# A hybrid convolution and state-space layer on one core: input sums and splits moved behind PSUM reads, and the last columns in two groups

## The chip, the cores and the metric

The kernel runs on one core of a Trainium2 chip. Time is device microseconds (us) of one execution; the median of three runs is quoted. Five engines work side by side, each through its own queue in order: TensorE (PE, with its weight loads as PEld), VectorE (DVE), ScalarE (ACT), GpSimd (POOL) and SyncE (SP), which here issues all DMAs.

## The reference, cut to what matters

One layer, for a prompt of 2048 tokens and a sample of 64, in fp32:

```python
h = rmsnorm(x, norm_in_w) * (1 + scale[:, None]) + shift[:, None]
proj = h @ w_in                       # 1024 -> 7184 columns
b_gate, c_gate, h_a, g_a, z, xbc_raw, dt_raw = jnp.split(proj, idx, axis=-1)
...                                   # short gated convolution -> y_a; chunked scan -> y_b
out = jnp.concatenate([y_a, y_b], axis=-1) @ w_out
x = x + gate[:, None] * out
y = rmsnorm(x, norm_f_w)
```

Outputs are y for both sequences and the final states of the convolutions and of the scan.

## The kernel before

**Two phases.** `phase_project` computes `h @ w_in` channel by token: 7 Strassen products in place of 8 block products, each operand split into a high and a low part (hi, lo in the one-pass fp32 format), so that a product is three matmuls. `phase_mix` then goes through 16 chunks of 128 prompt tokens (and the sample first): the scan, the output projection, the residual and the final norm.

**Items and slots.** `work` lists items, each 256 columns of w_in; items 0 to 27 are the first pass (tokens 0 to 1023, 512 columns to a matmul), items 28 to 55 the second (the other 1088 tokens, two units of 272 columns). An item has seven slots, one for each product; (24,2) is slot 2 of item 24. A slot's matmuls are 12 of 512 columns in the first pass, 24 of 272 in the second. The quarters and sums of the input that the products multiply (A11, S1, S2, S4, S3, A12, A22 for slots 0 to 6) stay in SBUF for a whole pass as tiles hi and lo, and are replaced for the second pass while item 27 and the first slots of item 28 run.

**What a slot issues,** in this order: its matmuls; activations that were due (`run_later`); the cast of the next item's weights (`w_hi`, ScalarE); the functions that `hooks` lists for the slot; some of the convolutions' work (`run_bg`); the low part of those weights and the next weight sums (`w_lo`, VectorE, one to three instructions, L233); then `evac`, the reads of PSUM: slots 0, 1, 2 into `keep` (ScalarE, L301), slots 3, 4, 5 added to `keep` (VectorE, L309), slot 6 (ScalarE, L307); then a function that `behind` lists. The order of a queue is the order of the code.

**Who waits for a PSUM read.** The matmuls of slot 2 add to the bank that slot 0 filled, so they wait for its `keep`; so slot 3 for slot 1 and slot 4 for slot 2. Slot 6 needs the bank read in slot 4. In the second pass slot 5 takes the banks read in slot 3, and slot 0 the banks read in slot 6 of the item before; unit 1 of (28,0) takes the bank that (27,6) leaves.

**Sums of the input.** `sums_in(i)` loads four blocks (tiles h_q) of one half of the channels from DRAM; `sums_step(i, n)` makes one sum on VectorE (L849, 128 x 1088) and stores it (hq_d). Both halves are done in items 23 to 25. `second_in(j, r)` loads what product j needs (tiles t_q, from hs_d or hq_d); `second(j)` casts it (two casts of 128 x 1088 on ScalarE, L171) and subtracts (two on VectorE, L172), then issues the load for product j+3.

**The last chunk.** Each chunk ends with `out_mm` for two halves of 512 columns; `take_b` scales, gates and adds each half (three VectorE instructions) and squares it with a sum (ScalarE); `end_rms` makes the root of the mean (VectorE, POOL), and `scale_out` multiplies all 1024 columns by it and by the final weight in one instruction (L1466), and stores them (L1467). For chunks but the last this runs beside the next chunk's work; after the last nothing is left to run beside it.

Of the kernel before, what the change touches and what calls it, by code (L numbers as in the profile page):

```python
# [8 lines left out]
F32 = mybir.dt.float32  # L9
F32R = mybir.dt.float32r  # L10
AF = mybir.ActivationFunctionType
ALU = mybir.AluOpType
# [15 lines left out]
def kernel(  # L28
# [8 lines left out]
    PE, ACT, DVE, POOL, SP = nc.tensor, nc.scalar, nc.vector, nc.gpsimd, nc.sync  # L37
# [3 lines left out]
    y_prompt, y_sample = y_prompt[0], y_sample[0]  # L41
# [35 lines left out]
    stats = pool(ctx, "stats", bufs=4)  # L77
# [16 lines left out]
    def rsqrt_mean(ss, n, out):  # L94
        ms = stats.tile([128, 1], F32, tag="ms", name="ms")
        DVE.tensor_scalar(out=ms[:n], in0=ss, scalar1=1.0 / D, scalar2=EPS, op0=ALU.mult, op1=ALU.add)
        POOL.tensor_tensor(out=out, in0=ms[:n], in1=mhalf[:n], op=ALU.pow)

    wo = {}

    def phase_project():
# [668 lines left out]
        def hook_at(t, fn):  # L770
            hook(t // 7, t % 7, fn)
# [55 lines left out]
        for gi in range(4):  # L827
            t0 = 19 * 7 + 1 + 8 * gi
# [8 lines left out]
        blocks = {}  # L837

        def sums_in(i):
            for n, (k0, o) in enumerate(((0, 0), (0, 544), (4, 0), (4, 544))):  # L840
                t = row(2 + n, [128, 2, 544], "h_q")
                SP.dma_start(out=t, in_=hs_d[:, k0 + 2 * i:k0 + 2 * i + 2, o:o + 544])
                blocks[n] = t

        def sums_step(i, n):
            a11, a21, a12, a22 = (blocks[x] for x in range(4))
            out, x, y, op = ((a22, a21, a22, ALU.add), (a21, a11, a21, ALU.subtract),
                             (a11, a22, a11, ALU.subtract), (a12, a12, a11, ALU.subtract))[n]
            DVE.tensor_tensor(out=out, in0=x, in1=y, op=op)  # L849
            SP.dma_start(out=hq_d[n, :, 2 * i:2 * i + 2, :], in_=out)  # L850

        for i, t0 in enumerate((23 * 7 + 6, 24 * 7 + 5)):
            hook_at(t0, lambda i=i: sums_in(i))
            for n in range(4):
                hook_at(t0 + 3 + n, lambda i=i, n=n: sums_step(i, n))

        tm = {}
        SOURCE = {"A11": (hs_d, 0, 0), "A12": (hs_d, 4, 0), "A22": (hs_d, 4, 544),
# [10 lines left out]
        def second(j):  # L869
            hi, lo = h_tile(PRODS[j], 544)  # L870
            for i, t in enumerate(tm.pop(j)):
                split(t, hi[:, 2 * i:2 * i + 2, :], lo[:, 2 * i:2 * i + 2, :])
            if j + 3 < 7:
                second_in(j + 3, (6, 2, 4)[j % 3])
# [1 line left out]
        hook(26, 0, lambda: second_in(0, 6))  # L876
        hook(26, 1, lambda: second_in(1, 2))
        hook(26, 2, lambda: second_in(2, 4))
        behind = {}
        for j, t, late in ((0, 1, 0), (1, 2, 0), (2, 4, 1), (3, 5, 1), (4, 6, 0), (5, 7, 0), (6, 9, 0)):  # L880
            if late:
                behind[27, t] = lambda j=j: second(j)
            else:
                hook_at(27 * 7 + t, lambda j=j: second(j))

        hook(30, 0, lambda: dt_project(1, 2))
        hook(30, 2, lambda: dt_gather(1))
# [49 lines left out]
        o = 0  # L937
        for ap in (conv_a_w[0], norm_a_w, conv_b_w[0], conv_b_b, norm_b_w, norm_in_w):
            n = ap.shape[0] * ap.shape[1] // 128
# [36 lines left out]
        for h, xs in enumerate(first):  # L976
            ss = x_ss()
            for i, (off, n, t) in enumerate(xs):
                ACT.activation(out=stage["A22"][:, 2 * (i % 2):2 * (i % 2) + 2, :].rearrange("p k t -> p (k t)"), in_=t,
                               func=AF.Square, accum_out=ss[:, i, 0:1])  # L980
# [150 lines left out]
        for n, (q, j) in enumerate((("A12", 3), ("A22", 3), ("A12", 2), ("A22", 2))):  # L1131
            plain_product(1, q, j)
            s4, t = (("S4", S), ("S3", S3))[n // 2]
# [92 lines left out]
        for g in range(2, last):  # L1226
            p = int(g >= NP0)
            slot_us = 2.75 if p == 0 else 3.05
            for s in range(7):
                now[0] = 7 * g + s  # L1230
                open_banks(p, g, s)
                product(p, g, s)
                run_later()
                if s == 1:
                    w_load(g + 2)
                if s == 2:
                    work[g][1]["begin"](p)
                tg, tj = (g, 6) if s == 0 else (g + 1, s - 1)
                if tg < last:
                    w_hi(tg, tj)  # L1240
                for fn in hooks.get((g, s), ()):
                    fn()
                cost = (W_COST[tj] if tg < last else 0.7) + (0.7 if 3 <= s <= 5 else 0.0) + (0.2 if p and s >= 3 else 0.0)
                credit = min(credit + slot_us - cost, slot_us)
                credit = run_bg(credit)
                if tg < last:
                    w_lo(tg, tj)
                elif s > 0:
                    last_w(s - 1)
                evac(p, g, s)  # L1250
                if (g, s) in behind:
                    behind[g, s]()
                if s == 4:
                    work[g][1]["done"](p, 1)
                if s == 6:
                    work[g][1]["done"](p, 0)
# [28 lines left out]
    def decay(c, hf):  # L1285
        h0, rb = hf * 8, loads[c, hf][1]
        lt = mix["sp1"].tile([128, 8, 128], F32, tag="lt", name="lt", bufs=2)
        for h in range(8):
            ACT.activation(out=lt[:, h, :], in_=rb[:, h, :], func=AF.Relu, scale=-1.0, bias=acum[:, c, h0 + h:h0 + h + 1])  # L1289
        ACT.activation(out=lt, in_=lt, func=AF.Exp, scale=-1.0)  # L1290
        held[c, hf] = lt

    def phase_mix():
        stack = ExitStack()
        psum = pool(stack, "ps2", bufs=5, space=bass.MemoryType.PSUM, reuse_waits="tile")
        sp = mix["sp"] = pool(stack, "sp", bufs=1, reuse_waits="tile")

        def bank(tag):
            return psum.tile([128, 512], F32, tag=tag, name=tag, bufs=5 if tag == "sd" else 3)
# [150 lines left out]
        def take_b(c, nn, t, ps, r, xr, ss):  # L1450
# [3 lines left out]
            DVE.tensor_tensor(out=xr[:n, s], in0=xr[:n, s], in1=t[:n], op=ALU.add)  # L1454
            ACT.activation(out=t[:n], in_=xr[:n, s], func=AF.Square, accum_out=ss[:n, nn:nn + 1])  # L1455

        def end_rms(c, ss):
            n = ntok(c)
            DVE.tensor_tensor(out=ss[:n, 0:1], in0=ss[:n, 0:1], in1=ss[:n, 1:2], op=ALU.add)
            rf = stats.tile([128, 1], F32, tag="rf", name="rf")  # L1460
            rsqrt_mean(ss[:n, 0:1], n, rf[:n])
            return rf
# [7 lines left out]
        n, va = NS_TOK, mix["va"]  # L1470
# [18 lines left out]
        vbh = split_act(vb, n, "vbh")  # L1489
# [4 lines left out]
        t0 = take_a(16, pa, ra)  # L1494
# [12 lines left out]
        t1 = take_a(16, pa, ra)  # L1507
# [8 lines left out]
        xr = prefetch_x(16)  # L1516
        gate = sp.tile([128, D], F32, tag="gate", name="gate")
        nf = sp.tile([128, D], F32, tag="nf", name="nf")
        SP.dma_start(out=gate, in_=g_d[1].partition_broadcast(128))
        SP.dma_start(out=nf, in_=norm_f_w.partition_broadcast(128))  # L1520
        ss = stats.tile([128, 2], F32, tag="fs", name="fs", bufs=2)
# [17 lines left out]
        pending = ends(16, t1, pb, rbs, xr, ss)  # L1539
        xr = prefetch_x(0)  # L1540
        for c in range(16):
            n, nxt, nx2 = 128, c + 1, c + 2
            more = nxt < 16
            vb = vb_of.pop(c)
            vbh = split_act(vb, n, "vbh")
            if more:
                prefetch(nxt, 1)
                prefetch_z(nxt, 1)
            if pending:
                pending[0]()  # L1550
            if more:
                va = prefetch_va(nxt)
                ssd1(nxt, 0)
            ra = inv_rms(sqa, n, "ra")
            if pending:
                pending[1]()
            split_dve(vb, n, vbh)
            square(vb, n)
            if pending:
                pending[2]()  # L1560
            sqb = sum_sq(vb, n, "vbh")
            if c == 0:
                SP.dma_start(out=gate, in_=g_d[0].partition_broadcast(128))
            if more:
                xr_next = prefetch_x(nxt)
            if not more:
                store_state()
            pa = out_mm(vah, 0, c, 0)
            if more:
                ssd2(nxt, 0)  # L1570
                decay(nxt, 1)
            t0 = take_a(c, pa, ra)
            if more:
                join1(nxt, 0)
                ssd1(nxt, 1)
                join2(nxt, 0)
                if nx2 < 16:
                    prefetch(nx2, 0)
                    prefetch_z(nx2, 0)
            pa = out_mm(vah, 0, c, 1)  # L1580
            rb_ = inv_rms(sqb, n, "rb")
            if more:
                ssd2(nxt, 1)
            t1 = take_a(c, pa, ra)
            if more:
                vah = split_act(va, n, "vah")
                split_dve(va, n, vah)
                square(va, n)
                join1(nxt, 1)
                sqa = sum_sq(va, n, "vah")  # L1590
                join2(nxt, 1)
                if nx2 < 16:
                    decay(nx2, 0)
            ss = stats.tile([128, 2], F32, tag="fs", name="fs", bufs=2)
            pb0 = out_mm(vbh, 8, c, 0)
            take_b(c, 0, t0, pb0, rb_, xr, ss)
            pb1 = out_mm(vbh, 8, c, 1)

            pending = ends(c, t1, pb1, rb_, xr, ss)
            if more:  # L1600
                xr = xr_next
        for f in pending:
            f()
        stack.close()

    with tc.manual_schedule():
# [30 lines left out]
```

## Time and profile before

| | |
|---|---|
| median of 3 runs | 1771.92 us (1771.9 to 1772.29) |
| the profiled execution, its own time | 1769.35 us |
| its span | 1767.5 us |
| busy share of the span | PE 97%, DVE 74%, ACT 47%, POOL 6% |
| chain of work that ended last | PE 86%, DVE 5%, DMA 4%, ACT 3% |
| lines of that chain | L276 (products) 54%, L1430 and L1437 (output projection) 21% |

The profile is of one execution. Busy time counts matmuls from start to end, and they overlap, so 97% does not mean that the engine runs at its peak; what matters is where it is not fed. The chain is followed back from the last instruction to what released each step.

### The profile page before, as it was taken

The page shows a single profiled execution, that of the slowest core. Times are in us where ns is not written, and L with a number is a line of the kernel's source. Part 1 is how long each engine was busy: PE and PEld are TensorE (multiplying, and loading weights), DVE is VectorE, ACT ScalarE, POOL GpSimd, SP SyncE. Part 2 cuts the span into 40 slices and gives each one's busy share as a digit, 9 for nine tenths or more (in the row PEclk, how much of TensorE's full clock was granted, in tenths as well). Part 3 has the DMA queues.
Part 4 walks back from the last instruction along what each step waited for, and adds up shares of the span by engine and source line. Part 5 has one row for each costly group of instructions (what it writes and reads, how often), then busy time and mean ns, then how long its engine had stood idle before and what let it go on. Part 6 is the DMA issues. An engine that isn't in the chain of part 4 may idle for free.

```text
span 1767.5 us, 26974 instructions
## 1 busy us (share of the span) xinstructions
PE 1716.4 (97%) x10561; PEld 1512.3 (86%) x10561; DVE 1306.8 (74%) x2019; ACT 826.9 (47%) x1575; POOL 102.5 (6%) x224
## 2 busy tenths in 40 slices
PE   5999999999999999999999999999899999999997
PEld 4788888887887799999999999999588888888886
DVE  5787779766576646678768767646788888888885
ACT  5644344444653645434333443325455555545551
POOL 0000000000000000001001000000011111101011
PEclk9999999999999999999999999999899999999999
DMA  9222323232548742322322242324653343434341
GB/s 338 72 76 92 96 84 102 89 107 86 170 151 287 248 123 61 91 74 76 113 82 73 74 119 79 113 90 143 213 179 139 137 150 125 160 107 169 108 149 36
DMA packets 186722, 220.20 MB, mean 125 GB/s; under 512 B 21300, under 2 KB 152356, under 8 KB 186596
## 3 DMA queue, kind: packets, MB, share of 16 engines
q1 hardware_dynamic: 186596, 218.49, 38.2%
q8 instruction: 83, 1.36, 0.3%
q14 instruction: 43, 0.35, 0.1%
HBM read 164.31 MB, written 54.15 MB: 124 GB/s over the span
## 4 chain that ended last, share of the span: by engine, by line
PE 86%; DVE 5%; DMA 4%; ACT 3%; issue 2%; SPq 0%; POOL 0%; POOLq 0%; DVEq 0%; ACTq 0%
PE bank L276 54%; PE mm L1430 14%; PE mm L1437 7%; PE sd L1355 2%; PE sd L1359 2%; PE sd L1361 2%; PE sd L1327 1%; DMA h_q<-hs_d 1%; PE sd L1331 1%; DMA praw<-in_w_mod_dram 1%; PE bank L1041 1%; DVE w L233 1%; DMA hq_d<-h_q 0%; DMA xt<-in_x_prompt_dram 0%; PE bank L530 0%
## 5 line engine op out<-in xcount | busy, mean ns | idle before, releaser
L276 PE MATMUL bank<-hiS,w 128*128 128x272 f32 (+1 forms) x2560 | 598.8, 323 | 9.6 <-ACT keep L301 9.5
L276 PEld LDWEIGHTS bank<-hiS,w 128*128 128x128 f32 x2560 | 432.4, 189 | 46.4 <-ACT keep L301 13.0
L276 PE MATMUL bank<-hiA,w 128*128 128x272 f32 (+1 forms) x1920 | 448.9, 322 | 5.8 <-DVE z_row L309 2.4
L276 PE MATMUL bank<-loS,w 128*128 128x272 f32 (+1 forms) x1280 | 412.4, 322 | 0.0
L276 PEld LDWEIGHTS bank<-hiA,w 128*128 128x128 f32 x1920 | 322.8, 188 | 34.7 <-DVE z_row L309 3.3
L233 DVE TENSOR_TENSOR w<-raw,w 128x512 fp32r<-128x512 f32 x318 | 217.9, 688 | 160.0 <-ACT w L242 149.0
L242 ACT CAST w<-raw 128x512 fp32r<-128x512 f32 x318 | 196.1, 622 | 256.7 <-PE bank L276 131.2
L276 PE MATMUL bank<-loA,w 128*128 128x272 f32 (+1 forms) x960 | 308.2, 321 | 0.0
L276 PEld LDWEIGHTS bank<-loS,w 128*128 128x128 f32 x1280 | 242.2, 189 | 15.8
L276 PEld LDWEIGHTS bank<-loA,w 128*128 128x128 f32 x960 | 180.5, 188 | 11.9
L301 ACT COPY keep<-bank 128x272 f32<-128x272 f32 (+1 forms) x240 | 105.9, 450 | 130.7 <-PE bank L276 130.2
L382 DVE SCALAR_TENSOR_TENSOR acc<-raw_row,par,acc 128x1024 f32<-128x1024 f32 (+1 forms) x96 | 126.5, 1318 | 2.0
L233 DVE TENSOR_TENSOR raw<-raw 128x512 f32<-128x512 f32 x161 | 111.0, 690 | 3.7
L1430 PE MATMUL mm<-woh,vbh 128*128 128x512 f32 (+1 forms) x272 | 110.0, 404 | 0.0
L1430 PE MATMUL mm<-woh,vah 128*128 128x512 f32 (+1 forms) x272 | 109.4, 402 | 0.0
L1430 PE MATMUL mm<-wol,vbh 128*128 128x512 f32 (+1 forms) x272 | 106.6, 392 | 0.0
L1430 PE MATMUL mm<-wol,vah 128*128 128x512 f32 (+1 forms) x272 | 106.4, 391 | 0.0
L1289 ACT ACTIVATE lt<-rb,acum 128x128 f32<-128x128 f32 x240 | 73.4, 388 | 3.5 <-DMA rb<-r_d 3.1
L242 ACT CAST w<-t 128x512 fp32r<-128x512 f32 x53 | 32.8, 618 | 74.1 <-PE bank L276 74.1
L1437 PE MATMUL mm<-woh,vbh 128*128 128x512 f32 (+1 forms) x272 | 67.2, 389 | 0.0
L1437 PE MATMUL mm<-woh,vah 128*128 128x512 f32 (+1 forms) x272 | 67.2, 389 | 0.0
L1455 ACT ACTIVATE t<-xr 128x512 f32<-128x512 f32 (+1 forms) x34 | 21.5, 633 | 92.9 <-DVE xr L1454 92.9
(282 smaller groups left out, 2381.8 us busy)
## 6 DMA issues: line engine op xcount, KB each, us to landing
raw<-in_w_in_dram SPq DMA_DIRECT2D x56, 1024.0 KB
xb_d<-acc SPq DMA_DIRECT2D x32, 512.0 KB
xb<-xb_d SPq DMA_DIRECT2D x32, 512.0 KB
rb<-r_d SPq DMA_DIRECT2D x30, 512.0 KB
xt<-in_x_prompt_dram SPq DMA_DIRECT2D x16, 512.0 KB
praw<-in_w_mod_dram SPq DMA_DIRECT2D x16, 512.0 KB
z_d<-z_row SPq DMA_DIRECT2D x16, 512.0 KB
va_d<-c_row SPq DMA_DIRECT2D x16, 512.0 KB
```

The lines of the kernel that those rows point to most:

```text
L233: DVE.tensor_tensor(out=out, in0=a, in1=b, op=ALU.subtract)
L242: ACT.copy(out=w[:, 0], in_=w_src(g, j))
L276: PE.matmul(ps[:, 0:n], w[:, a, k, :], h[:, k, o:o + n], start=(s in (0, 1, 5) and k == 0 and i == 0), stop=(k == 3 and i == 2), skip_grou ...
L301: ACT.copy(out=keep[s][:, o:o + n], in_=b["y" if s == 1 else "x"][:, 0:n])
L382: DVE.scalar_tensor_tensor(out=acc[:, 0:n], in0=r[:, k:k + n], scalar=cb_w(k, t), in1=acc[:, 0:n], op0=ALU.mult, op1=ALU.add)
L1289: ACT.activation(out=lt[:, h, :], in_=rb[:, h, :], func=AF.Relu, scale=-1.0, bias=acum[:, c, h0 + h:h0 + h + 1])
L1355: PE.matmul(py4[64 * e:64 * e + 64, j, :], xd[:, 2 * j + e, :], lt[:, 2 * j + e, :], start=True, stop=True)
L1359: PE.matmul(po4[:, j, :], state[:, hf, j * 128:(j + 1) * 128], xb[:, 6 + j // 2, :], start=True, stop=True)
L1361: PE.matmul(ps[:, g * 256:(g + 1) * 256], bc[:, g, :], xe[:, 4 * g:4 * g + 4, :].rearrange("p h q -> p (h q)"), start=True, stop=True)
L1430: PE.matmul(ps[:n], hl[:, 0, k, 0:n], wo[k0 + k][i][:, nn * 512:(nn + 1) * 512], start=(k == 0 and i == 0), stop=False)
L1437: PE.matmul(ps[:n], hl[:, 1, k, 0:n], wo[k0 + k][0][:, nn * 512:(nn + 1) * 512], start=False, stop=(k == 7))
L1455: ACT.activation(out=t[:n], in_=xr[:n, s], func=AF.Square, accum_out=ss[:n, nn:nn + 1])
```

## The change

The sums and all seven splits now run behind the slot's PSUM reads, by `behind`, which takes several functions for a slot. The second set of sums is loaded one slot later, and its four steps run in slots (25,4), (25,5), (25,6) and (26,0) instead of (25,1) to (25,4). The last chunk has a function of its own, `last_out`: its 1024 columns are multiplied in groups of 512, 256 and 256, multiplied by the final weight before the root is known, then scaled by the root on VectorE (first half) and ScalarE (two quarters), and stored in two halves.

```diff
         def sums_step(i, n):
-            a11, a21, a12, a22 = (blocks[x] for x in range(4))
+            a11, a21, a12, a22 = (blocks[i, x] for x in range(4))
...
+        behind = {}
+
+        def behind_at(t, fn):
+            behind.setdefault((t // 7, t % 7), []).append(fn)
+
-        for i, t0 in enumerate((23 * 7 + 6, 24 * 7 + 5)):
+        for i, (t0, wait) in enumerate(((23 * 7 + 6, 3), (24 * 7 + 6, 5))):
             hook_at(t0, lambda i=i: sums_in(i))
             for n in range(4):
-                hook_at(t0 + 3 + n, lambda i=i, n=n: sums_step(i, n))
+                behind_at(t0 + wait + n, lambda i=i, n=n: sums_step(i, n))
...
-        behind = {}
-        for j, t, late in ((0, 1, 0), (1, 2, 0), (2, 4, 1), (3, 5, 1), (4, 6, 0), (5, 7, 0), (6, 9, 0)):
-            if late:
-                behind[27, t] = lambda j=j: second(j)
-            else:
-                hook_at(27 * 7 + t, lambda j=j: second(j))
+        for j, t in enumerate((1, 2, 4, 5, 6, 7, 9)):
+            behind_at(27 * 7 + t, lambda j=j: second(j))
...
                 evac(p, g, s)
-                if (g, s) in behind:
-                    behind[g, s]()
+                for fn in behind.get((g, s), ()):
+                    fn()
...
+        def last_out(c, hl, t0, t1, r, xr):
+
+            ss = stats.tile([128, 4], F32, tag="fl", name="fl", bufs=1)
+            t2 = sp.tile([128, 4, 64], F32, tag="et", name="t2").rearrange("p a b -> p (a b)")
+            groups = ((0, 512, t0), (512, 256, t1[:, 0:256]), (768, 256, t1[:, 256:512]))
+            for i, (o, w, t) in enumerate(groups):
+                s = slice(o, o + w)
+                ps = bank("mm")
+                for part in range(2):
+                    for k in range(8):
+                        for a in range(2 - part):
+                            PE.matmul(ps[:, 0:w], hl[:, part, k, :], wo[8 + k][a][:, s],
+                                      start=(part == 0 and k == 0 and a == 0), stop=(part == 1 and k == 7))
+                DVE.scalar_tensor_tensor(out=t, in0=ps[:, 0:w], scalar=r, in1=t, op0=ALU.mult, op1=ALU.add)
+                DVE.tensor_tensor(out=t, in0=t, in1=gate[:, s], op=ALU.mult)
+                DVE.tensor_tensor(out=xr[:, s], in0=xr[:, s], in1=t, op=ALU.add)
+                ACT.activation(out=t, in_=xr[:, s], func=AF.Square, accum_out=ss[:, i:i + 1])
+                if i < 2:
+                    DVE.tensor_tensor(out=xr[:, s], in0=xr[:, s], in1=nf[:, s], op=ALU.mult)
+                else:
+                    DVE.tensor_tensor(out=t2, in0=xr[:, s], in1=nf[:, s], op=ALU.mult)
+                if i:
+                    DVE.tensor_tensor(out=ss[:, 0:1], in0=ss[:, 0:1], in1=ss[:, i:i + 1], op=ALU.add)
+            rf = stats.tile([128, 1], F32, tag="rf", name="rf")
+            rsqrt_mean(ss[:, 0:1], 128, rf)
+            y = y_prompt[c * 128:c * 128 + 128, :]
+            DVE.tensor_scalar(out=xr[:, 0:512], in0=xr[:, 0:512], scalar1=rf, scalar2=None, op0=ALU.mult)
+            SP.dma_start(out=y[:, 0:512], in_=xr[:, 0:512])
+            for o, src in ((768, t2), (512, xr[:, 512:768])):
+                ACT.activation(out=xr[:, o:o + 256], in_=src, func=AF.Copy, scale=rf)
+            SP.dma_start(out=y[:, 512:1024], in_=xr[:, 512:1024])
...
+            if not more:
+                last_out(c, vbh, t0, t1, rb_, xr)
+                break
```

Where it moves instructions, the queues show it. VectorE from the last weight part of (25,0) to the PSUM read of (25,4), with w, t and raw the weight part, h_q a sum and z_row a PSUM read. Before:

```order
L233 TENSOR_TENSOR w_4310<-raw,w_4310 128x512
L849 TENSOR_TENSOR h_q<-h_q 128x1088
L233 TENSOR_TENSOR w_4332<-raw,w_4332 128x512
L233 TENSOR_TENSOR t_4337<-raw 128x512
L233 TENSOR_TENSOR raw<-raw 128x4x128
L849 TENSOR_TENSOR h_q<-h_q 128x1088
L233 TENSOR_TENSOR w_4356<-raw,w_4356 128x512
L233 TENSOR_TENSOR raw<-raw 128x4x128
L849 TENSOR_TENSOR h_q<-h_q 128x1088
L233 TENSOR_TENSOR w_4376<-raw,w_4376 128x512
L309 TENSOR_TENSOR z_row<-bank_4316,keep_4362 128x512
L849 TENSOR_TENSOR h_q<-h_q 128x1088
```

The same stretch of VectorE's queue now:

```order
L233 TENSOR_TENSOR w_4310<-raw,w_4310 128x512
L233 TENSOR_TENSOR w_4332<-raw,w_4332 128x512
L233 TENSOR_TENSOR t_4335<-raw 128x512
L233 TENSOR_TENSOR raw<-raw 128x4x128
L233 TENSOR_TENSOR w_4354<-raw,w_4354 128x512
L233 TENSOR_TENSOR raw<-raw 128x4x128
L233 TENSOR_TENSOR w_4372<-raw,w_4372 128x512
L309 TENSOR_TENSOR z_row<-bank_4316,keep_4358 128x512
L233 TENSOR_TENSOR w_4388<-raw,w_4388 128x512
L309 TENSOR_TENSOR z_row<-bank_4297,keep_4338 128x512
L849 TENSOR_TENSOR h_q<-h_q 128x1088
```

The four sums have left the slots (25,1) to (25,4) up to the second PSUM read; the first stands behind that read.

ScalarE from the weight cast of (27,6) to the first PSUM copy of (28,0) and, after, the cast pair behind it; hiS and hiA are cast pairs of the input, w a weight cast, z_row at L307 the copy of (27,6), keep a PSUM copy. Before:

```order
L242 CAST w_4745<-raw 128x512
L171 CAST hiS_4747<-t_q 128x1088 x2
L307 COPY z_row<-bank_4579 128x512
L332 ACTIVATE z_row<-z_row 128x1024
L242 CAST w_4784<-raw 128x512
L171 CAST hiA_4786<-t_q 128x1088 x2
L301 COPY keep_4793<-bank_4756 128x272
```

The same stretch of ScalarE's queue now:

```order
L242 CAST w_4745<-raw 128x512
L307 COPY z_row<-bank_4579 128x512
L171 CAST hiS_4750<-t_q 128x1088 x2
L332 ACTIVATE z_row<-z_row 128x1024
L242 CAST w_4784<-raw 128x512
L301 COPY keep_4787<-bank_4756 128x272
L301 COPY keep_4787<-bank_4757 128x272
L171 CAST hiA_4790<-t_q 128x1088 x2
```

Each cast pair has changed places with the PSUM copy of its slot.

VectorE from the weight part of (28,1) to the PSUM read of (28,3), with loA the subtractions of product 6. Before:

```order
L233 TENSOR_TENSOR w_4824<-raw,w_4824 128x512
L233 TENSOR_TENSOR t_4827<-raw 128x512
L233 TENSOR_TENSOR raw<-raw 128x4x128
L172 TENSOR_TENSOR loA_4862<-t_q,hiA_4861 128x1088 x2
L233 TENSOR_TENSOR w_4859<-raw,w_4859 128x512
L233 TENSOR_TENSOR raw<-raw 128x4x128
L233 TENSOR_TENSOR w_4896<-raw,w_4896 128x512
L309 TENSOR_TENSOR z_row<-bank_4796,keep_4869 128x272
```

The same stretch of VectorE's queue now:

```order
L233 TENSOR_TENSOR w_4824<-raw,w_4824 128x512
L233 TENSOR_TENSOR t_4827<-raw 128x512
L233 TENSOR_TENSOR raw<-raw 128x4x128
L233 TENSOR_TENSOR w_4859<-raw,w_4859 128x512
L233 TENSOR_TENSOR raw<-raw 128x4x128
L172 TENSOR_TENSOR loA_4867<-t_q,hiA_4866 128x1088 x2
L233 TENSOR_TENSOR w_4896<-raw,w_4896 128x512
L309 TENSOR_TENSOR z_row<-bank_4796,keep_4863 128x272
```

The two subtractions have moved behind the weight part of (28,2) and still stand ahead of the PSUM read of (28,3).

## Rows read from the trace of the kernel before

**Rows 1.** The page, busy time, share and instructions of each engine.

```profile
PE 1716.4 (97%) x10561; PEld 1512.3 (86%) x10561; DVE 1306.8 (74%) x2019; ACT 826.9 (47%) x1575; POOL 102.5 (6%) x224
```

**Rows 2.** Windows: length; busy us of PE, PEld, DVE, ACT, POOL; PEclk; DMA share; GB/s.

```profile
523.98:585.24 61.26, 58.06 (x254) 47.07 (x253) 40.89 (x55) 22.86 (x37) 0.00 (x0) 1.00 0.88 303
585.24:633.03 47.79, 42.81 (x254) 38.43 (x252) 35.12 (x46) 30.87 (x44) 0.00 (x0) 0.96 0.57 183
```

**Rows 3.** The chain that ended last: start, us, what.

```profile
497.52 16.36 PE bank L276 x72
...
626.91 30.33 PE bank L276 x240
```

**Rows 4.** Timeline of PEld: start, us, what, idle before it and its releaser.

```profile
541.44 0.19 PEld L276 LDWEIGHTS bank<-hiA,w 128*128 128x128 f32 x1 [1.40 <-DVE b_row L309]
...
557.27 0.19 PEld L276 LDWEIGHTS bank<-hiS,w 128*128 128x128 f32 x1 [2.37 <-ACT keep L301]
563.30 0.19 PEld L276 LDWEIGHTS bank<-hiA,w 128*128 128x128 f32 x1 [0.69 <-DVE z_row L309]
...
597.91 0.19 PEld L276 LDWEIGHTS bank<-hiS,w 128*128 128x128 f32 x1 [2.05 <-ACT keep L301]
...
609.95 0.19 PEld L276 LDWEIGHTS bank<-hiA,w 128*128 128x128 f32 x1 [2.23 <-ACT z_row L307]
622.73 0.19 PEld L276 LDWEIGHTS bank<-hiS,w 128*128 128x128 f32 x1 [0.65 <-ACT keep L301]
626.91 0.19 PEld L276 LDWEIGHTS bank<-hiA,w 128*128 128x128 f32 x1 [1.14 <-DVE z_row L309]
```

**Rows 5.** Timeline of VectorE, items 24 and 25.

```profile
534.08 1.29 DVE L849 TENSOR_TENSOR h_q<-h_q 128x1088 f32<-128x1088 f32 x1 [4.02 <-DMA h_q<-hs_d]
...
540.69 0.69 DVE L309 TENSOR_TENSOR b_row<-bank,keep 128x512 f32<-128x512 f32 x1
...
555.34 0.69 DVE L233 TENSOR_TENSOR raw<-raw 128x512 f32<-128x512 f32 x1
```

**Rows 6.** Timeline of ScalarE, items 25 to 28.

```profile
556.12 0.62 ACT L242 CAST w<-raw 128x512 fp32r<-128x512 f32 x1 [5.55 <-DVE raw L233]
...
588.64 0.62 ACT L242 CAST w<-raw 128x512 fp32r<-128x512 f32 x1
...
607.32 2.10 ACT L171 CAST hiS<-t_q 128x1088 fp32r<-128x1088 f32 x2
609.32 0.57 ACT L307 COPY z_row<-bank 128x512 f32<-128x512 f32 x1
...
615.59 0.66 ACT L301 COPY keep<-bank 128x272 f32<-128x272 f32 x2
```

**Rows 7.** The chain that ended last, the second load of h_q.

```profile
546.21 6.58 DMA h_q<-hs_d
```

**Rows 8.** Windows, the stretch of the splits; columns as in rows 2.

```profile
590.29:626.90 36.61, 31.64 (x183) 28.12 (x181) 30.07 (x36) 23.97 (x34) 0.00 (x0) 0.95 0.63 208
```

**Rows 9.** Timeline of VectorE, the subtractions of product 6.

```profile
621.43 2.49 DVE L172 TENSOR_TENSOR loA<-t_q,hiA 128x1088 fp32r<-128x1088 f32 x2 [1.69 <-ACT hiA L171]
```

**Rows 10.** A window of PE alone: length, busy, PEclk, DMA share, GB/s.

```profile
610.00:615.00 5.00, 5.00 (x28) 0.66 1.08 380
```

**Rows 11.** Groups of VectorE by form: xcount, busy us, mean ns.

```profile
L1336 DVE TENSOR_TENSOR bc<-sd,cst 128x256 f32<-128x256 f32 x32 | 13.5, 422 | 17.4 <-ACT bc L1335 17.4
...
L1011 DVE TENSOR_SCALAR stA<-stA,scol,bcol 128x512 f32<-128x512 f32 x10 | 5.3, 542 | 0.0
```

**Rows 12.** Timeline of VectorE and SP's queue at the end.

```profile
1758.47 0.75 DVE L1452 SCALAR_TENSOR_TENSOR t<-mm,rb,t 128x512 f32<-128x512 f32 x1 [3.20 <-PE mm L1437]
...
1762.47 1.28 DVE L1466 SCALAR_TENSOR_TENSOR xr<-xr,rf,nf 128x1024 f32<-128x1024 f32 x1 [0.66 <-POOL rf L97]
1763.78 0.34 SPq L1467 DMA_DIRECT2D out_dram<-xr  x1
```

**Rows 13.** Windows, the last store; columns as in rows 2.

```profile
1764.50:1766.10 1.60, 0.00 (x0) 0.00 (x0) 0.00 (x0) 0.00 (x0) 0.00 (x0) 0.50 0.82 328
```

More of the change, by code (lines that the diff above doesn't have):

```diff
@@ L842, in sums_in @@
                 SP.dma_start(out=t, in_=hs_d[:, k0 + 2 * i:k0 + 2 * i + 2, o:o + 544])
-                blocks[n] = t
+                blocks[i, n] = t
         def sums_step(i, n):
-            a11, a21, a12, a22 = (blocks[x] for x in range(4))
+            a11, a21, a12, a22 = (blocks[i, x] for x in range(4))
             out, x, y, op = ((a22, a21, a22, ALU.add), (a21, a11, a21, ALU.subtract),
@@ L1599, in phase_mix @@
             pending = ends(c, t1, pb1, rb_, xr, ss)
[L1600 to L1603, printed above, removed]
+            xr = xr_next
         stack.close()
```

## The prediction, made before the result was known

> **What bounds the kernel now.** I read the page first: TensorE is busy 97% of the span and VectorE 74% [rows 1]. Time can only come out of places where TensorE is not fed, so next I took the stretch the edits touch, from slot (24,0), which starts at 523.98, in two windows [rows 2]. A fed slot of the first pass is 72 matmuls in 16.36 us for six slots, 2.73 us; one of the second pass is 240 matmuls in 30.33 us for ten, 3.03 us [rows 3]. Slots (24,0) to (26,6) should take 21 x 2.73 = 57.3 us and take 61.26; slots (27,0) to (28,6) should take 7 x 2.73 + 7 x 3.03 = 40.3 and take 47.79. So 4.0 and 7.5 us are lost there, 11.5 in all. That is the most the first part of the change can give.
>
> The timeline of weight loads names the seven waits [rows 4], 10.5 us of idle in all: a PSUM bank that ScalarE (keep, z_row at L307) or VectorE (b_row, z_row at L309) has not read yet. Their timelines say why. On VectorE the first sum of the input, L849, waits 4.02 us for its DMA; the reads behind it in the queue are late, and the copy of (24,4) starts at 540.69 only [rows 5]. At the second set of sums the same stall reaches ScalarE by a detour: a weight cast waits 5.55 us for a raw tile whose update on VectorE (555.34) stands behind the sum [rows 5, 6], and the PSUM copy behind that cast frees the bank for (25,4). In item 27 the detour is shorter: pairs of casts of the input stand directly ahead of PSUM copies, as 2.10 us at 607.32 ahead of the copy at 609.32 [rows 6].
>
> **Sums.** Nothing is removed: the eight L849 and their eight stores stay. The first four move behind the reads of the same slot. In (24,2) the weight part of (25,1), 1.2 us in all, now passes ahead of the sum that waits for DMA, and in (24,4) the PSUM read precedes its sum, 1.29 us [rows 5]. So that read starts some 2.4 us earlier than at 540.69 and is done at 539.0, before (24,6) asks for the bank, at 541.44 less its wait of 1.40 [rows 4], 540.0. The second four go from slots (25,1) to (25,4) to (25,4) to (26,0). Their data are asked for one slot later, land about 555 (the last load took 6.58 us from 546.21 [rows 7], and is now issued 1 to 2 us later), and are used after (25,4) ends at 556.6; VectorE finds them there. SP's queue: the spill of c_row now goes ahead of the second load, the stores of the second sums go behind z_row's spills, and the t_q loads of products 1 and 2 wait for those stores, to about 571. They are cast at 590 at the earliest, so some 19 us, less a load's 6.58, cover this; the weight load behind them has until 584. I take all three waits of items 24 and 25 as gone: **-4.0 us** (bounds: -1.3 if only the first set is cured, -4.1).
>
> **Splits.** Each pair of casts and pair of subtractions now follows the PSUM copies of its slot, as those of products 2 and 3 did already. What comes late next: the weight cast behind the pair, and by it VectorE's weight part. I followed both queues from (27,0), which starts at 585.24 - 4.0 = 581.2. Between 590.29 and 626.90 VectorE executed fourteen subtractions, seventeen weight operations and the PSUM reads up to the one that released (28,5): 30.07 us busy, 6.5 us idle [rows 8]. The same list is needed after. It can begin earlier, with the weight part of (28,0): its cast at 588.64 lies 3.4 us behind the start of (27,0) and takes 0.62 [rows 6], so VectorE starts at 585.3. By the cast rows (0.62, and 2.10 a pair) it then idles 1.2 us for the first pair, about 0.7 for one weight cast, 0.5 elsewhere, since ScalarE is now ahead of it almost everywhere; the 1.69 us before loA at 621.43 [rows 9] shrinks to 0.3, because the weight part of (29,1) goes first. So the read for (28,5) is done at 585.3 + 30.1 + 2.4 = 617.8. TensorE would ask for it at 581.2 + 7 x 2.73 + 5 x 3.03 = 615.5. Hence **2.3 us of waiting stays** in the split stretch, some 0.6 at (28,4) and the rest at (28,5), now for want of VectorE time, not of order. Then (29,0) starts at 617.8 + 2 x 3.03 = 623.9, and it starts at 633.0 now: **-9.1 us** for sums and splits together (bounds: -5 if VectorE's idle time stays at 6.5, -11.5 if no wait is left).
>
> The clock: the granted clock fell once here, to a mean of 0.66 in 610 to 615 [rows 10], that is to 1.2 GHz for part of it, after waits of 2.05 and 2.23 us. It hid: (28,2) needed the first half of the copy at 615.59 [rows 6], done 0.1 us before (28,2) began at 616.08. So losing that drop gives about 0.1, and I add nothing.
>
> **Last chunk.** 24 matmuls of 512 columns become 48 of 256. The trace has no such pair at this speed; a line through 512 (16.36/72 = 227 ns) and 272 (30.33/240 = 126 ns) [rows 3] gives 119 ns, so 48 x 119 - 24 x 227 = +0.26 us. Bounds 0 and +0.6 (126 each). The Trainium skill, "TensorE: Matmul & The Clock Gate", section "Back-to-back issue gap", gives N/2.4 + 2.5 ns, 109 ns for 256: 48 of them would cost an estimated +0.06 us against 24 by its own 216 ns, and the sum below would be 0.2 better; the rows of this trace lie above its line for 512, so the row's value stands.
>
> VectorE now starts on the second half at 1758.47 [rows 12]. After, the last quarter is ready at 1758.7, but VectorE is still in the first quarter (the multiplication by the final weight waits for ScalarE's square of the same columns) and reaches it at about 1759.1. Three steps of 256 at 422 ns [rows 11], a square and the sum give the root some 0.35 us earlier than now. Behind it stand half of the columns as one tensor_scalar (542 ns for a costlier one [rows 11]) with ScalarE beside it on two quarters, instead of 1.28 us at 1762.47 [rows 12]; the second store is issued near 1762.95, now 1763.78: -0.8. The bytes in flight last are half: the store moves 512 KB in 1764.5 to 1766.1 [rows 13], so -0.5. Together **-1.3 us**, PE's +0.26 included. Bounds: 0 (twice as many packets, each no quicker) and -1.6.
>
> **Sum.** -9.1 - 1.3 = -10.4 us. The profiled execution took 1769.35 us for a span of 1767.5; it would take 1759.0, with a span of 1757.1. The median of the runs lies 2.57 us above the profiled one; I keep that distance: **1761.5 us**, 0.6% faster. A measurement of this kernel can tell about 0.2%, 3.5 us, from no change.
>
> **Rivals.**
> - *VectorE bound throughout.* Items 24 and 25 are cured, but in the splits the idle time of VectorE only changes place; -4.0 - 1.0 - 1.3 = 1765.6. For it: 30.07 of 36.61 us busy [rows 8]. Against: its longest idle times stood before the casts that move. Chance 0.13.
> - *The clock falls again, unhidden.* The waits left at (28,4) and (28,5) come close together. If it falls behind them, the row of the present fall gives the price: 28 matmuls in 5 us where 5/0.126 = 40 fit [rows 3, 10], 12 x 0.126 = 1.5 us: 1763.0. Against: after 2.37 and 0.69 us within six us (557 and 563) it did not fall [rows 4]. Chance 0.12. [...] Falls elsewhere may also come out otherwise by the earlier start; the range has 1.5 us for that either way.
> - *All waits gone*, if VectorE's queue is faster than I make it: -11.5 - 1.3 = 1759.1. Chance 0.12.
> - *Slower: late weights.* The second sums' stores go out seven us later against the slots, and the t_q loads that wait for them hold SP's queue ahead of a weight load. If that weight tile, needed from 584 (item 28's first cast), landed after 594, ten us would be lost and the gain with it; at 1 us for each beyond 584, 598 gives 1775. It needs loads of over 20 us where an h_q load took 6.58 [rows 7]; for it, the DMA engines are 88% busy there [rows 2]. Chance 0.03.
> - *The order changes, the time not*, since another reader of the same banks ends as late: 1770. Chance 0.05.
>
> My forecast has the remaining 0.55. Faster by over 0.2% (below 1768.4): forecast, clock, all gone, VectorE bound: 0.92, less a little for several terms failing at once, 0.90. Same 0.06, slower 0.04. Range 1758.0 to 1766.0: it holds the first four cases but for the edges of the clock, and leaves out about 2 in 10. The likeliest one's own range is 1759.5 to 1763.5.
>
> **What would show it.** Right: no wait of TensorE over 0.3 us from (24,0) to (28,2), one or two waits summing to 2 to 2.5 us at (28,4) and (28,5), for keep and z_row; VectorE idle under 3 us from (27,1) to (28,3); (29,0) near 624; two last stores, the second issued 0.8 us earlier against the end of the matmuls; span 1757. Wrong: a wait at (25,4) or (27,4) still there; a t_q or weight cast that waits for DMA; the clock at half in 612 to 620; a last store that ends no sooner. I would be most wrong by the 2.4 us of VectorE idle time in the splits, on which 4 us hang.

## The result, and the profile after

The change made the kernel slower: 1781.57 us median (1780.92 to 1782.85, 4 runs) against 1771.91 (1771.45 to 1772.29, 4 runs), a ratio of 1.0055 with a 95% interval of 1.0039 to 1.0071. The forecast was 1761.5 us. The profiled execution has a span of 1779.8 us, where 1757 was expected.

The page's first line, to be read beside [rows 1]: VectorE and ScalarE work 1.3 and 2.2 us more than before, TensorE is busy 21.2 us longer, and only 24 matmuls were added.

```profile
PE 1737.6 (98%) x10585; PEld 1514.1 (85%) x10585; DVE 1308.1 (73%) x2026; ACT 829.1 (47%) x1579; POOL 101.4 (6%) x224
```

So nothing new is waited for; the matmuls themselves come more slowly. The chain that ended last says where (start, us, what):

```profile
86.95 325.04 PE bank L276 x1392
...
508.36 16.80 PE bank L276 x72
532.51 79.97 PE bank L276 x343
...
630.32 30.39 PE bank L276 x240
...
705.35 349.58 PE bank L276 x2784
```

A 512-column matmul of the first pass takes 16.80/72 = 233 ns; it took 227 [rows 3]. The row at 86.95 shows it from the first item on, 325.04/1392 = 233.5 ns, some 450 us ahead of the first instruction that the diff moves. The 272-column matmuls hardly differ: 30.39 us for 240, before 30.33 [rows 3].

The stretch that the edits touch, (24,0) to (27,0) and (27,0) to (29,0), has the columns of [rows 2]; under it stands, from the timeline of weight loads, the one wait for a PSUM bank that the table of waits has for TensorE there:

```profile
535.15:593.95 58.80, 58.80 (x254) 47.34 (x252) 41.21 (x55) 22.95 (x37) 0.00 (x0) 1.00 0.89 306
593.95:636.43 42.48, 41.00 (x253) 36.96 (x252) 34.93 (x46) 30.45 (x44) 0.00 (x0) 1.00 0.69 219
```

```profile
630.32 0.19 PEld L276 LDWEIGHTS bank<-hiA,w 128*128 128x128 f32 x1 [1.70 <-DVE z_row L309]
```

The reader is to see two things at once. The waits of [rows 4] are gone but for one at (28,5), so the moved reads do what was forecast of them: 61.26 and 47.79 us became 58.80 and 42.48. And those 58.80 us are 21 slots of 2.80 us with no gap, where a fed slot was 2.73 [rows 3].

On VectorE the first sum still waits for its DMA, 1.84 us now and 4.02 in [rows 5], but the weight work and the reads of `b_row` stand ahead of each sum or between two:

```profile
545.21 1.29 DVE L849 TENSOR_TENSOR h_q<-h_q 128x1088 f32<-128x1088 f32 x1 [1.84 <-DMA h_q<-hs_d]
546.42 0.69 DVE L233 TENSOR_TENSOR w<-raw,w 128x512 fp32r<-128x512 f32 x1
547.03 0.68 DVE L309 TENSOR_TENSOR b_row<-bank,keep 128x512 f32<-128x512 f32 x1
547.63 1.28 DVE L849 TENSOR_TENSOR h_q<-h_q 128x1088 f32<-128x1088 f32 x1
```

### The profile page after: what moved, and what is told of

Its sections match the earlier page's. It is cut to its first block, busy times and chain, and to the rows that moved or that the text cites. A ratio compares the mean times of both kernels' runs of the same rounds, so it can differ in the third digit from the quotient of the medians.

```text
span 1779.8 us, 27034 instructions
## 1 busy us (share of the span) xinstructions
PE 1737.6 (98%) x10585; PEld 1514.1 (85%) x10585; DVE 1308.1 (73%) x2026; ACT 829.1 (47%) x1579; POOL 101.4 (6%) x224
## 4 chain that ended last, share of the span: by engine, by line
PE 92%; ACT 2%; DVE 2%; DMA 2%; issue 1%; SPq 0%; POOL 0%; POOLq 0%; ACTq 0%; DVEq 0%
PE bank L276 58%; PE mm L1431 14%; PE mm L1438 7%; PE bank L1042 3%; PE sd L1356 2%; PE sd L1360 2%; PE sd L1362 2%; PE sd L1328 1%; PE sd L1332 1%; DMA praw<-in_w_mod_dram 1%; DMA xt<-in_x_prompt_dram 0%; PE bank L529 0%; PE bank L530 0%; PE bank L820 0%; PE sd L1330 0%
## 5 line engine op out<-in xcount | busy, mean ns | idle before, releaser
L1431 PE MATMUL mm<-woh,vbh 128*128 128x512 f32 (+1 forms) x256 | 104.4, 408 | 0.0
L1431 PE MATMUL mm<-wol,vbh 128*128 128x512 f32 (+1 forms) x256 | 101.1, 395 | 0.0
L1438 PE MATMUL mm<-woh,vbh 128*128 128x512 f32 (+1 forms) x256 | 64.9, 395 | 0.0
L1438 PEld LDWEIGHTS mm<-woh,vah 128*128 128x128 f32 (+1 forms) x272 | 50.3, 185 | 13.2
```

The costliest lines, as they stand in the source:

```text
L1431: PE.matmul(ps[:n], hl[:, 0, k, 0:n], wo[k0 + k][i][:, nn * 512:(nn + 1) * 512], start=(k == 0 and i == 0), stop=False)
L1438: PE.matmul(ps[:n], hl[:, 1, k, 0:n], wo[k0 + k][0][:, nn * 512:(nn + 1) * 512], start=False, stop=(k == 7))
```

## The experiments

What differs from the first item on can't be the order of items 24 to 28. One line of the diff reaches that far: `last_out` takes its sums of squares from a new tile, `fl`, of the pool `stats`. That pool is opened before `lp` and `sp`. In the table of places that the program gives its tiles, `fl` (four numbers, 16 bytes) takes 32 bytes of each partition, and everything in `lp` and `sp` lies 32 bytes higher. The stationary operands, which a matmul has loaded ahead of it, are among them: `w0` to `w6` of the products and `vah`, `vbh` of the output projection. The moving operands, which are streamed past them (`hi..`, `lo..`, `woh..`, `wol..`), are laid out from the other end of SBUF and stay.

```
byte in the partition    w0      hiS2    hiS2 - w0         vah     woh0    woh0 - vah
before                   31072   108384  302 x 256         35552   73696   149 x 256
changed kernel           31104   108384  302 x 256 - 32    35584   73696   149 x 256 - 32
```

**1. The change without the new tile.** The tag `fs` is made four columns wide, which fits in the bytes that it takes already:

```diff
-            ss = stats.tile([128, 4], F32, tag="fl", name="fl", bufs=1)
+            ss = stats.tile([128, 4], F32, tag="fs", name="fs", bufs=2)
...
-            ss = stats.tile([128, 2], F32, tag="fs", name="fs", bufs=2)
+            ss = stats.tile([128, 4], F32, tag="fs", name="fs", bufs=2)
```

> The change whole, but the sums of squares of the last chunk lie in the pool's existing tag fs (made four columns wide, within the bytes it already takes), so that every tile keeps the place in SBUF that it has in the kernel before. Theory A (places): the change moved all tiles of lp and sp (the weights w0 to w3 among them) 32 bytes up, because its new tile fl takes 32 bytes of the stats pool, and that made the 512-column matmuls of L276, L1431 and L1438 slower, 227 to 233 ns. Then they are at 227 ns here, and the time is the 1781.6 of the change less about 23.7 us (12.3 us of longer span and 11.4 us that the moved reads and the last chunk gained): 1758, span 1756. Theory B (order or code): the moved casts and sums, or the added instructions, slow TensorE: 233 ns stay and the time is 1780 to 1783. Theory C: the gain of the edits is smaller than it looks and part of the slowness is theirs: 1762 to 1768.

Measured: 1758.46 us (1757.05 to 1759.24) against 1771.1, ratio 0.9928 [0.9915, 0.994], faster than both kernels. The chain, the windows of the two stretches, and the two weight loads that waited:

```profile
92.29 310.65 PE bank L276 x1368
...
692.10 348.80 PE bank L276 x2784
```

```profile
523.77:580.89 57.12, 57.12 (x253) 47.30 (x252) 41.36 (x55) 23.12 (x37) 0.00 (x0) 1.00 0.89 307
580.89:623.22 42.33, 40.63 (x253) 36.91 (x252) 34.92 (x46) 30.47 (x44) 0.00 (x0) 1.00 0.73 231
```

```profile
612.32 0.19 PEld L276 LDWEIGHTS bank<-hiS,w 128*128 128x128 f32 x1 [0.42 <-ACT keep L301]
...
617.09 0.19 PEld L276 LDWEIGHTS bank<-hiA,w 128*128 128x128 f32 x1 [1.72 <-DVE z_row L309]
```

310.65/1368 = 227.1 ns: with the places restored the old rate is back, in the same order of instructions. Theory A holds; theories B and C are out.

The 23.7 us between the two spans (1779.8 and 1756.1) are then, nearly whole: 2184 matmuls of the first pass at 233.5 less 227.1 ns, 14.0 us; 16 chunks of the output projection at 30.89 less 30.34, 8.8 us; and the 0.8 us between the two rows of 2784 matmuls. That makes 23.6. A chunk's period is read from the chain, the changed kernel's first, then this one's:

```profile
1409.78 3.84 PE mm L1431 x16
...
1440.67 3.84 PE mm L1431 x16
```

```profile
1422.89 3.76 PE mm L1431 x16
...
1453.23 3.76 PE mm L1431 x16
```

**2 to 4. The kernel before with nothing but other places.** One unused tile in each kernel, of 32 bytes in `stats` (stationary operands 32 bytes up), of 64 bytes there, and of 32 bytes at the other end (moving operands 32 bytes down):

```diff
     stats = pool(ctx, "stats", bufs=4)
+    stats.tile([128, 4], F32, tag="fl", name="fl", bufs=1)
...
+    stats.tile([128, 16], F32, tag="fl", name="fl", bufs=1)
...
+    rpad = pool(ctx, "rpad", side="right")
+    rpad.tile([128, 8], F32, tag="rp", name="rp")
```

> The kernel before with one unused tile of 32 bytes in the stats pool: no instruction is added or moved, the tiles of lp and sp lie 32 bytes higher. Theory A: the 512-column matmuls go from 227 to 233 ns in both parts of the kernel, the 272-column ones stay at 125 to 126; about 1771.9 + 23 = 1795 us. Theory B: 1772, 227 ns. Theory C: between, 1776 to 1785.

> The kernel before with one unused tile of 64 bytes: the tiles of lp and sp lie 64 bytes higher. Theory A with a period of 64 bytes in the weights' address: 227 ns, 1772 us. Theory A with a longer period (128 bytes or more), or any shift against the other operand: 233 ns, near 1795. Theory B: 1772.

> The kernel before with an unused tile of 32 bytes on the other side of SBUF: the moving operands (hiA, hiS, loA, loS, woh, wol) lie 32 bytes lower, the weights stay where they are. If what counts is how the moving operand's address stands to the stationary one's, as e2: 233 ns, near 1795. If the stationary operand's address alone counts: 227 ns, 1772. If the moving operand's alone counts: also another rate than 227 ns here, though e2 would then have kept 227. Theory B: 1772.

Measured: 1791.21, 1792.42 and 1791.6 us against 1771.1; ratios 1.0113 [1.0099, 1.0127], 1.0117 [1.0101, 1.0132] and 1.0114 [1.01, 1.0128]. Theory A gave some 3 us too much (1795). The chain of the first and of the third:

```profile
87.70 325.03 PE bank L277 x1392
...
713.93 349.58 PE bank L277 x2784
```

```profile
88.17 325.03 PE bank L278 x1392
...
715.64 349.57 PE bank L278 x2784
```

One edit moves the stationary operands and the other the moving ones, and the rows agree to 0.01 us: that fits the distance between the two, not the place of either, and runs 6 and 7 test it. That 64 bytes are no better than 32 rules out a period of 64.

**5. Seven distances in one kernel.** An unused tile ahead of each of `w0` to `w6` gives each slot a distance of its own; it is counted here as stationary less moving, modulo 256 bytes:

```diff
+        for j in range(7):
+            lp.tile([128, 8 if j else 24], F32, tag=f"pad{j}", name=f"pad{j}")
+            lp.tile([128, 2, 4, 128], F32R, tag=f"w{j}", name=f"w{j}")
```

> The kernel before with unused tiles ahead of w0 to w6, so that the weight tile of each of the seven slots lies at another distance from the moving operands (stationary address less moving address, modulo 256 bytes): w0 96, w1 128, w2 160, w3 192, w4 224, w5 0, w6 32; the mix phase lies as before. Theory A, only the same place modulo 256 counts: slot 5 at 227 ns for its 512-column matmuls, the other six at 231 to 235; about 13 us slower in the first pass, 1784 us. A period of 128 bytes: slot 1 at 227 too. A distance that is better than that of the kernel before: some slot clearly under 227 ns. Theory A', only the stationary operand's own place counts: the result of the right-hand shift already speaks against it; then w0 to w6 would differ in no way that follows the distance.

Measured: 1781.27 us (2 runs), ratio 1.0058 [1.0037, 1.0078]. From the first matmul of a slot to the first of the next, over 12, median of fourteen items of the first pass: 233.9, 232.2, 233.6, 229.9, 232.8, 227.3 and 233.0 ns for distances of 96, 128, 160, 192, 224, 0 and 32 bytes. The timeline of PE in slots 5 and 6 of item 7 shows it by every third matmul (those of `loA`):

```profile
199.41 0.39 PE L279 MATMUL bank<-loA,w 128*128 128x512 f32 x1
...
200.09 0.39 PE L279 MATMUL bank<-loA,w 128*128 128x512 f32 x1
...
200.77 0.39 PE L279 MATMUL bank<-loA,w 128*128 128x512 f32 x1
...
202.84 0.40 PE L279 MATMUL bank<-loA,w 128*128 128x512 f32 x1
...
203.54 0.40 PE L279 MATMUL bank<-loA,w 128*128 128x512 f32 x1
...
204.24 0.40 PE L279 MATMUL bank<-loA,w 128*128 128x512 f32 x1
```

Three matmuls take 0.68 us in slot 5 and 0.70 in slot 6. Only the distance 0 gives 227 ns; 128 does not, 192 is between, and none is better than the kernel before. The 272-column matmuls of the second pass have four distances in every kernel, because their moving rows are 2176 bytes apart. In the trace of before their mean steps, without the longest 5%, are 125.1, 126.0, 126.0 and 123.6 ns for 0, 64, 128 and 192 bytes: there 0 is not the quickest.

**6 and 7. Two shifts that cancel.** Weights 224 bytes up and moving operands 32 down in the kernel before; and, with `fl` left in the changed kernel, moving operands 224 down:

```diff
+    stats.tile([128, 56], F32, tag="fl", name="fl", bufs=1)
+    rpad = pool(ctx, "rpad", side="right")
+    rpad.tile([128, 8], F32, tag="rp", name="rp")
...
+    rpad = pool(ctx, "rpad", side="right")
+    rpad.tile([128, 56], F32, tag="rp", name="rp")
```

> The kernel before with both sides shifted: the tiles of lp and sp (weights) 224 bytes up, the moving operands 32 bytes down. Either shift alone by 32 bytes cost 20 us. Theory A with a period of 256 bytes in the distance: the distance is a multiple of 256 again, 227 ns, 1771 us like the kernel before. If each operand's own place counts, or the period is longer than 256 bytes: 231 to 235 ns, 1791.

> The changed kernel with its tile fl left as it is, and an unused tile of 224 bytes on the other side, so that the moving operands lie 224 bytes lower and the distance is a multiple of 256 again. Theory A: 227 ns, 1758 us like the run in which fl lay in an existing tag. If the tile fl cost time in another way than by the distance: 1781.

Measured: 1771.35 us against 1771.1, ratio 0.9998 [0.9988, 1.0008], and 1759.37, ratio 0.9936 [0.9921, 0.9951]. The chain of each:

```profile
93.99 310.62 PE bank L279 x1368
```

```profile
92.46 310.65 PE bank L278 x1368
```

The 32 bytes that cost 20 us alone (run 4) cost nothing once the distance is a multiple of 256 bytes again, and the changed kernel is mended without touching a line of the change.

**8 to 10. Each edit alone, places as before.** The sums; the splits (`behind[27 + t // 7, t % 7]` for all seven); the last chunk with its sums in `fs`.

> The kernel before with the change's first edit alone: the sums of the input behind the PSUM reads, the second four one slot later; splits, last chunk and all addresses as before. By the prediction's term for the sums, -4.0 us: 1767, with (26,0) reached 4 us earlier and nothing given back in items 26 to 29. Rival, the sums only pay together with the splits since VectorE is the bound behind them: under 2 us, 1769 to 1771.

> The kernel before with the change's second edit alone: the splits of products 0, 1, 4, 5 and 6 behind the PSUM reads of their slot; sums, last chunk and addresses as before. The prediction's terms give 9.1 less 4.0, -5.1 us: 1766 against 1771.1, with the stretch from (27,0) to (29,0) at 42.7 instead of 47.8 us. Rival, VectorE is the bound there and its idle time only changes place: -1.0 us, 1770. If the three edits add up (the run of all three without the new tile gave 12.6, the sums alone 6.7), 1766 to 1767.

> The kernel before with the last chunk's edit alone, its sums of squares in the existing tag fs, so that every address stays. The prediction's term, -1.3 us: 1769.8, with the last store issued 0.8 us earlier after the start of the last chunk's output products, and the end of that store 1.3 us earlier. Rival, two groups of 256 columns cost TensorE more than the halved tail gives back: 0 to +0.5 us, 1771 to 1771.6.

Measured: 1764.4 us (0.9965 [0.9952, 0.9978]), 1764.71 (0.9966 [0.9953, 0.9979]) and 1769.82 (0.999 [0.9982, 0.9999]). That is 0.35, 0.34 and 0.10%, together 0.79% beside 0.72% for all three (interval 0.60 to 0.85): they add up. The windows from (24,0) to (27,0) and from (27,0) to (29,0) of the sums alone, then the second of them of the splits alone:

```profile
522.98:580.10 57.12, 57.12 (x254) 47.31 (x252) 41.35 (x55) 23.12 (x37) 0.00 (x0) 1.00 0.89 307
580.10:627.88 47.78, 41.49 (x253) 36.91 (x252) 35.10 (x46) 30.87 (x44) 0.00 (x0) 1.00 0.65 205
```

```profile
584.92:627.28 42.36, 40.66 (x254) 36.94 (x252) 34.93 (x46) 30.51 (x44) 0.00 (x0) 1.00 0.65 206
```

Each cures its own stretch as in run 1, without the other. "VectorE is the bound" was wrong for both. The last chunk alone is faster by 0.1%, with an interval that reaches nearly to none.

## Why the prediction was wrong

**The step that failed is the cost of what the change adds.** The part on the last chunk prices the new groups, steps and store, and says nothing of the tile `fl` that they need. The sum is made with the 227 ns of [rows 3] for all that isn't mentioned. Both rest on the unspoken assumption that an allocation costs nothing: the term was 0 and it is +23.7 us of span, or 23.1 us between the medians (the changed kernel against run 1). None of the rivals was this one. "Slower: late weights" had the right sign, but no load was late: in that stretch the only wait for a DMA on VectorE is the first sum's 1.84 us. Nothing in the trace of before showed the price: its 512-column products of the steady stream all have the one distance, and the 272-column ones, which have four, differ by 2.4 ns at most and not in favour of the multiple of 256. The tile could be seen in the diff, and its place in the program; that the place costs time needed a run.

The other steps are judged by run 1, where that term is taken out. It gave 1758.46 us for a forecast of 1761.5, with a span of 1756.1 for 1757.1. So the edits gave 1.0 us more than forecast; the other 2.0 us are the distance between the median and the profiled execution, which the forecast kept at 2.57 us and which is 0.54 in run 1 (1758.46 less 1757.92).

- **Sums, -4.0.** 61.26 [rows 2] became 57.12: -4.1. Right, in size and place, and so was the "all three waits gone".
- **Splits, 2.3 us of waiting stay.** 0.42 at (28,4) and 1.72 at (28,5), 2.14 in all, for `keep` and `z_row` as named. The stretch went from 47.79 [rows 2] to 42.33, -5.5 where -5.1 was said. (29,0) starts at 623.2, forecast 623.9. VectorE's idle time, by which the forecast said it might err most, was under 3 us as said: 25.35 less 23.20 = 2.2 us from (27,1) to (28,3) of run 1:

```profile
583.61:608.96 25.35, 25.35 (x146) 22.54 (x144) 23.20 (x27) 21.45 (x30) 0.00 (x0) 1.00 0.88 275
```

- **The clock.** No fall: the granted clock is 1.00 in both stretches of run 1, with waits of 0.42 and 1.72 us 4.8 us apart. That the fall of before cost nearly nothing was right too: run 8 has the old splits and no fall from (27,0) to (29,0), a granted clock of 1.00 for 0.96 in [rows 2], and takes 47.78 us there instead of 47.79.
- **Last chunk, -1.3.** From the first product of the last group (1747.20, and 1736.96 in run 1) to the issue of the last store it took 16.58 us and takes 15.84: -0.74, forecast -0.8. To the end of the span it took 20.30 and takes 19.14: -1.2. The 256-column matmuls of run 1 come every 0.12 us, as the line through [rows 3] said. By the formula for the isolated gap in the Trainium skill, "TensorE: Matmul & The Clock Gate", section "Back-to-back issue gap", the estimate for 256 columns is 109 ns; these rows don't agree with it. The timelines of PE before, of PE in run 1, and of SP's queue there:

```profile
1747.20 0.47 PE L1430 MATMUL mm<-woh,vbh 128*128 128x512 f32 x1
```

```profile
1736.96 0.47 PE L1469 MATMUL mm<-woh,vbh 128*128 128x512 f32 x1
...
1743.00 0.28 PE L1469 MATMUL mm<-woh,vbh 128*128 128x256 f32 x1
1743.12 0.28 PE L1469 MATMUL mm<-wol,vbh 128*128 128x256 f32 x1
1743.24 0.28 PE L1469 MATMUL mm<-woh,vbh 128*128 128x256 f32 x1
```

```profile
1752.36 0.34 SPq L1485 DMA_DIRECT2D out_dram<-xr  x1
1752.80 0.38 SPq L1488 DMA_DIRECT2D out_dram<-xr  x1
```

The three stretches give 10.8 of the 11.4 us by which run 1's span is shorter than that of before; the other 0.6 us lie outside them.

So the profile of the changed kernel showed the local signs that were listed as "right" (no wait up to (28,2), VectorE fed, two last stores) or came near them (1.70 us of waiting where 2 to 2.5 was listed). The two that are counted from the start of the program failed: (29,0) at 636.4 instead of 624, and the span by over 22 us. No sign asked whether a stretch that nothing touched ran as before.

## What to carry to other kernels

A tile that is added to an early pool moved, in this program, every tile of the pools opened after it from the same end of SBUF. Where TensorE is the bound, look at the distance between the stationary and the moving operands before and after, and keep it: put the tile into an existing tag (run 1), or add bytes until the distance differs by a multiple of 256 (runs 6 and 7). And after a change compare the rate of a stretch that nothing touched first: one row of the chain (us by count) shows here that the loss is not where the edits are.

## What the runs showed of the hardware

- A 512-column matmul in the one-pass fp32 format (fp32r), of a steady stream, each with its own 128 x 128 weights, took 227 ns where the stationary and the moving operand lie a multiple of 256 bytes apart in the partition, and 230 to 234 ns at the seven other multiples of 32 (runs 2 to 5). The 272-column ones changed by 0.2 to 0.4% (2784 of them took 348.80 us in run 1, 349.58 in run 2, 350.32 in run 3). There the distance changes from matmul to matmul in any layout (run 5 above).
- The multiple of 256 is not best for every width. The 48 matmuls of 256 columns in the last chunk came every 118 ns in the changed kernel, 32 bytes off (16 steps between the two rows below), and every 120 ns in runs 1 and 7, at a multiple of 256.

```profile
1766.23 0.28 PE L1469 MATMUL mm<-woh,vbh 128*128 128x256 f32 x1
...
1768.12 0.28 PE L1469 MATMUL mm<-woh,vbh 128*128 128x256 f32 x1
```

- Why it is so stays open. In the trace the load of the next weights runs beside each matmul; that the reads of the two operands then get into each other's way would fit a rule on their distance. No run here takes the weight loads away, so this is argued and not shown.
- The clock fell in some executions of the old order where the profile of before has no fall. In runs 10 and 6, whose sums stand as before, the window from (24,0) to (27,0) has a mean granted clock of 0.97 (1.2 GHz for part of it), and 62.73 and 62.41 us instead of the 61.26 of [rows 2]. The other five runs with the old order of the sums (2, 3, 4, 5 and 9) have 1.00 there, and no profile with the sums moved was under it. What a fall alone costs there is not shown: runs 3 and 4 took 62.57 and 62.51 us without one, and the wait for `keep` that is 2.37 us in [rows 4] differs too. It was 3.26 us in run 10, 2.78 in run 6 and 3.19 in run 3, so its length does not tell where the clock falls. The windows of runs 10 and 6, and the weight loads behind that wait in runs 10 and 3:

```profile
524.15:586.88 62.73, 59.05 (x254) 48.13 (x252) 40.90 (x55) 22.90 (x37) 0.00 (x0) 0.97 0.87 296
```

```profile
525.41:587.82 62.41, 59.40 (x254) 48.29 (x253) 40.91 (x55) 22.86 (x37) 0.00 (x0) 0.97 0.86 298
```

```profile
558.20 0.29 PEld L276 LDWEIGHTS bank<-hiS,w 128*128 128x128 f32 x1 [3.26 <-ACT keep L301]
```

```profile
570.00 0.19 PEld L277 LDWEIGHTS bank<-hiS,w 128*128 128x128 f32 x1 [3.19 <-ACT keep L302]
```
